# The two gate projections of the forward scan as seven block products for each pair of chunks, with the block sums of the input and of the weights built in the backward pass

## The chip, the core and the metric

The kernel runs on one core of a Trainium2 chip. Its time is that of one execution on the device, in microseconds (us). The engines are named as in the profile: PE (TensorE, matmuls; PEld is its weight load), DVE (VectorE), ACT (ScalarE), POOL (GpSimd) and SP (SyncE, here a queue of DMAs alone). Each engine works through its own instructions in order.

## The reference

One layer of a bidirectional hybrid encoder over 4096 tokens of width 1024, batch 1. Cut to what matters here (`mlstm` stands for the chunkwise mLSTM of one direction, chunks of 128 tokens, 4 heads of 128):

```python
hn = rms_norm(x, norm_w)
qk_a, v_a, o_a, z_a, g_a, q_b, k_b, v_b, z_b = split(hn @ w_in)   # 1024, 512, 512, 512, 16, 512, 128, 128, 512
q_a, k_a = split(silu(centred_depthwise_conv(qk_a, conv_w, conv_b)))
h = sigmoid(o_a) * (mlstm(q_a, k_a, v_a, forward) + mlstm(q_a, k_a, v_a, backward))
h = h * rsqrt(mean(h * h, per head) + EPS) * mhn_w
y_a = h * silu(z_a)
y_b = windowed_gqa(q_b, k_b, v_b, sink, rel_bias) * silu(z_b)
out = rms_norm(x + concat(y_a, y_b) @ w_out, final_norm_w)
```

`o_a` is `hn` times columns 1536 to 2048 of `w_in`, `z_a` is `hn` times columns 2048 to 2560. These two are the gate projections that the change is about.

## The kernel before

Every matmul in float32 is made of three passes at a shorter format: an operand is split into a high part and a low remainder, and PE adds low by high, high by low and high by high into one bank of PSUM. The split costs two instructions, a copy that rounds (ACT) and a subtract (DVE, some on POOL).

The program has four stages.

**First pass** (to about 588 us). Norm, transposes, the windowed attention of group B. It leaves the normalised input, transposed and split, in DRAM as `xT_d`.

**Second pass, the backward scan** (`pass2`, to about 1167 us). Eight blocks of 512 tokens, from the last to the first, four chunks each. Per block PE does the v projection of the four chunks (96 matmuls of 128x512), then the K projections (m = 4 to 7, one for each head) and the Q projections (m = 0 to 3). Behind each of these eight, `qkproj` runs the convolution: ACT evicts into U (L936), POOL copies the four columns shared with the neighbouring block from and into a small tile `hl` (L944, L945), ACT takes the first tap (L948), DVE four more (L950), ACT the tanh (L952), DVE the product (L953). During the Q projections `place` mixes in the transposes of K (`ktp`, L991) and the updates of the state (`kvp`), which need weighed values: `weigh` forms them on POOL and DVE, half each (L1004), then ACT (L1006) and DVE (L1007). POOL also issues the transfers of the state to DRAM (`kf_d`, `cb_d`). The input of a block is eight tiles `xb`, loaded by SP during the block before.

**Third pass, the forward scan** (`pass3`, to about 1679 us). 32 chunks. For each, `proj` makes `op` and `zp`, two times eight K tiles times three matmuls of 128x512 (L1262), in two PSUM banks that take turns (tag `pj`). Behind `op`, ACT takes the tanh (L1270); behind `zp`, ACT the tanh and DVE a product with the bank (L1272). The operands are `xs` tiles, loaded for two chunks at a time from `xT_d`. Among these matmuls `interleave` spreads the scan's own pieces: `heads` (L1214, L1215, the numerators `num`), `yout` (L1249, the transposes `yp` of a chunk's finished heads `hs`), `scores` (L1190, S). `weigh_q` multiplies the weights W by q on DVE (L1204), `state` carries CC forward (L1197), `decays` masks and exponentiates E (POOL L1178, ACT L1182). From num to yp a chunk runs through DVE L1224 to L1226, ACT L1229, DVE L1230, L1234, ACT L1238, DVE L1239, POOL L1240 and DVE L1242.

**Tail.** The z gate of group B for blocks 0 to 7 (`zunits`; L158 to L160, block 0 inside chunk 31 of the scan), and from 1861 us the output projection, which already computes two row blocks by two column blocks with seven products in place of eight (L1443, sums at L1457).

The order on PE is that of the code. The order on the other engines is set by a scheduler with its own estimates; `tc.high_priority(offset=EV)` draws evictions forward, `behind` puts an instruction after another one. Tiles of one tag take turns in a fixed number of buffers, and a load waits until the last reader of its buffer is through. Tiles `x4` (`xtile`) and the weights `w8` (`wtile`) are such rings, shared by all stages.

## Time and profile before

| | us |
|---|---|
| runs | 2188.42, 2188.40, 2185.29; median 2188.40 |
| the profiled execution | 2188.4 |
| its span, first to last instruction | 2182.1 |
| second pass, from about | 588 to 1167 |
| one of its blocks | 74.5 |
| third pass, from about | 1167 to 1679 |
| output projection, PE | 1861.4 to 2172.7 |

The profile is one execution, with the busy time of each engine, tables by stretches of time, and groups of instructions by line, engine, tiles and shape (`out<-in`, partitions x elements, count, busy us, mean ns, then the idle time before them and who ended it). A chain of waits goes back from the last instruction. Line numbers are those of the kernel before.

### The profile page before, as it was taken

What the parts mean: (1) busy time and instruction counts of PE and PEld (TensorE: products, weight loads), DVE (VectorE), ACT (ScalarE), POOL (GpSimd) and SP (SyncE); (2) the same over time, 40 slices, a digit from 0 to 9 for tenths busy, and PEclk for the clock granted to TensorE, in tenths of its full rate; (3) what the DMA queues carried; (4) which work ended last, traced back from release to release, by engine and by line L of the source; (5) the groups of instructions that cost most, each with busy time, mean ns of one, the idle gap of its engine ahead of it and who ended that gap; (6) DMA issues with size and microseconds to landing.
All of it is one profiled execution on the core that took longest, in us unless ns stands there. A gap on an engine that the chain in (4) does not pass through costs nothing. (4 is left out here: it accounts for less than half of the span.)

```text
span 2182.1 us, 34919 instructions
## 1 busy us (share of the span) xinstructions
PE 2156.9 (99%) x12226; PEld 1872.4 (86%) x12226; DVE 1416.9 (65%) x3041; ACT 1079.3 (49%) x2650; POOL 567.7 (26%) x918
## 2 busy tenths in 40 slices
PE   8999999999999999999999999999999999999998
PEld 7999999999898888888888888888888888888886
DVE  7678787788686566556567655555554443777786
ACT  7788788787554344334344544444443321333333
POOL 3555465550031121121112211121211111112222
PEclk9999999999999999999999999999999999999999
DMA  9655455332342454144357887677676998667775
GB/s 277 158 171 147 128 173 122 130 124 64 102 148 78 141 163 135 62 160 160 113 163 230 290 259 238 211 253 225 214 238 188 329 359 283 181 177 191 193 191 147
DMA packets 249132, 398.96 MB, mean 183 GB/s; under 512 B 21979, under 2 KB 128475, under 8 KB 248956
## 3 DMA queue, kind: packets, MB, share of 16 engines
q1 hardware_dynamic: 220544, 303.50, 45.4%
q0 software_dynamic: 28176, 92.96, 13.6%
q8 instruction: 96, 1.57, 0.3%
q14 instruction: 80, 0.66, 0.1%
q10 hardware_dynamic: 236, 0.27, 0.1%
HBM read 275.99 MB, written 120.67 MB: 182 GB/s over the span
## 5 line engine op out<-in xcount | busy, mean ns | idle before, releaser
L932 PE MATMUL up<-xb,w 128*128 128x512 f32 x1344 | 338.4, 396 | 0.0
L1443 PE MATMUL o<-wo,yo 128*128 128x512 f32 (+1 forms) x1356 | 312.8, 393 | 0.0
L1443 PEld LDWEIGHTS o<-wo,yo 128*128 128x128 f32 x1356 | 253.2, 188 | 59.7
L932 PEld LDWEIGHTS up<-xb,w 128*128 128x128 f32 x1344 | 243.8, 188 | 47.2
L950 DVE SCALAR_TENSOR_TENSOR qk<-U,cw,qk 128x512 f32<-128x512 f32 x256 | 189.2, 752 | 91.1 <-ACT qk L948 85.8
L548 PE MATMUL qp<-xT,wqb 128*128 128x256 f32 x1536 | 242.4, 288 | 0.1
L548 PEld LDWEIGHTS qp<-xT,wqb 128*128 128x128 f32 x1536 | 214.2, 190 | 8.7 <-DVE wqb L319 0.5
L1262 PE MATMUL op<-w,xs 128*128 128x512 f32 x720 | 202.3, 408 | 0.0
L1262 PE MATMUL zp<-w,xs 128*128 128x512 f32 x720 | 187.9, 401 | 0.7 <-DVE z L1272 0.7
L905 PE MATMUL v2p<-w,xb 128*128 128x512 f32 x672 | 157.6, 395 | 0.0
L1262 PEld LDWEIGHTS zp<-w,xs 128*128 128x128 f32 x720 | 130.9, 189 | 27.4 <-DVE z L1272 1.1
L414 DVE TENSOR_TENSOR pt<-tp,pt 128x512 fp32r<-128x512 f32 x188 | 129.1, 687 | 37.7 <-ACT pt L413 35.2
L905 PEld LDWEIGHTS v2p<-w,xb 128*128 128x128 f32 x672 | 126.1, 188 | 30.1 <-DMA xb<-xT_d 0.5
L391 ACT ACTIVATE s<-s,NG 128x320 f32<-128x320 f32 (+1 forms) x256 | 139.8, 548 | 11.4 <-DVE NG L389 10.8
L1262 PEld LDWEIGHTS op<-w,xs 128*128 128x128 f32 x720 | 126.7, 189 | 21.4
L413 ACT CAST pt<-tp 128x512 fp32r<-128x512 f32 x188 | 110.5, 588 | 69.9 <-PE tp L411 67.6
L382 DVE CUSTOM_DVE_ANT_0 s<-sp,G 128x320 f32<-128x320 f32 (+1 forms) x256 | 122.2, 478 | 32.6 <-PE sp L379 29.9
L1229 ACT ACTIVATE hs<-num,r 128x128 f32<-128x128 f32 x128 | 47.0, 368 | 174.3 <-DVE r L1226 153.6
L425 PE MATMUL op<-pt,v 128*128 128x512 f32 x376 | 120.6, 402 | 5.9 <-DVE ab L438 5.8
L379 PE MATMUL sp<-kk,q 128*128 128x320 f32 (+2 forms) x512 | 118.8, 313 | 0.7 <-DVE kk L501 0.6
L411 PE MATMUL tp<-ident,s 128*128 128x128 f32 x752 | 113.2, 273 | 0.3 <-DVE pt L414 0.2
L1252 POOL DMA_DIRECT2D y_d<-ya x32 | 19.4, 607 | 329.8 <-ACT ya L1251 181.8
(275 smaller groups left out, 4480.5 us busy)
## 6 DMA issues: line engine op xcount, KB each, us to landing
xc<-xT_d SPq DMA_DIRECT2D x64, 512.0 KB, 8.1
xs<-xT_d SPq DMA_DIRECT2D x120, 256.0 KB, 6.6
xT_d<-xT POOLq DMA_DIRECT2D x104, 256.0 KB, 5.0
xb<-xT_d SPq DMA_DIRECT2D x48, 514.0 KB, 8.0
E<-m_d SPq DMA_DIRECT2D x64, 256.0 KB, 4.9
W<-w_d SPq DMA_DIRECT2D x64, 256.0 KB, 5.9
y<-y_d SPq DMA_DIRECT2D x32, 512.0 KB, 3.4
out<-xr POOLq DMA_DIRECT2D x31, 512.0 KB, 3.7
```

What stands on the lines that cost most here:

```text
L379: nc.tensor.matmul(sp[:, lo:hi], qt, kk[:, kv, z, col - 128 + lo:col - 128 + hi], start=(z == 0), stop=(z == 1))
L382: nc.vector.tensor_tensor_reduce(out=s[:, lo:hi], in0=sp[:, lo:hi], in1=bias[0][:, kv * 2 + m, lo - 64 * half:hi - 64 * half], op0=ALU.add ...
L391: LAST["act"] = nc.scalar.activation(ps[g][:, kept(g)], ps[g][:, kept(g)], AF.Exp, bias=ng[:, g:g + 1], accum_out=rs[:, g:g + 1])
L411: nc.tensor.transpose(tp[:, g * 128:(g + 1) * 128], ps[g][:, j * 128:(j + 1) * 128], c.ident)
L414: nc.vector.tensor_sub(pt[:, 1, :], tp, f32(pt[:, 0, :]))
L425: nc.tensor.matmul(op, vt, pt[:, z, :], start=(i == 0 and z == 0), stop=(i == len(js) - 1 and z == 1))
L548: nc.tensor.matmul(qp, wq[k // 2][:, k % 2, w, m * 128:m * 128 + 128], x[k], start=(k == 0 and j == 0), stop=(k == KT - 1 and j == 2))
L905: nc.tensor.matmul(vp, a, wv[k // 2][:, k % 2, m, :], start=(k == 0 and j == 0), stop=(k == KT - 1 and j == 2))
L932: nc.tensor.matmul(up[:, 0:hi - lo], w[k // 2][:, k % 2, a, cs], x, start=(k == 0 and j == 0), stop=(k == KT - 1 and j == 2))
L950: nc.vector.scalar_tensor_tensor(acc, U[:, t:t + 512], cw[:, cm, t:t + 1], acc, ALU.mult, ALU.add)
L1262: nc.tensor.matmul(P[nm], XS[n](a, k), w[:, m, :], start=(k == 0 and j == 0), stop=(k == KT - 1 and j == 2))
L1443: nc.tensor.matmul(p, a[:, z, k, :], w[k // 2][:, k % 2, m, lo:hi], start=k == 0 and z == 1, stop=k == 3 and z == 0 and m == 0)
```

## The change

For chunks 2j and 2j+1, K halves A (k = 0 to 3) and B (k = 4 to 7), the inputs x0A, x0B, x1A, x1B and the weights oA, oB, zA, zB form a product of two by two blocks. It is computed from seven products of one sum of inputs and one sum of weights each, 12 matmuls of 128x512 per product (4 K tiles, 3 passes):

| product | input | weight | added into |
|---|---|---|---|
| 0 | x0A | oA | copied |
| 1 | x1A + x1B - x0A | zB - zA + oA | u = P1 + P0 |
| 2 | x0B | oB | o of chunk 2j = P2 + P0 |
| 3 | x1A + x1B | zA - oA | z = P3 + u |
| 4 | x0A - x1A | zB - zA | z of chunk 2j+1 = P4 + z; u = P4 + u |
| 5 | x0B - x1A - x1B + x0A | zB | z of chunk 2j = P5 + z |
| 6 | x1B | oB - zB + zA - oA | o of chunk 2j+1 = P6 + u |

- Backward pass: `xunit`, eight times per block, forms the input sums on POOL (six adds, two of 256 columns and four of 128) and writes them to `xo_d` by a POOL transfer of 448 KB; `wunit`, four times in each of blocks 6 to 3, forms the weight sums (two SP loads, two ACT scalings, four POOL adds, one POOL transfer to `wt_d`). `opweights` loads and splits 14 weight tiles (ACT copy and DVE subtract of 128x1024 each), twelve of them in block 0, in place of eight tiles of `wgroup`. In block 0 the last two Q projections are now mixed as in the others.
- Forward scan: `pair` in place of `proj`, 42 matmuls per chunk; `op_load` and `op_split` load and split each input sum (ACT copy; subtract on DVE for even products, on POOL for odd ones). `evict` copies P0 on ACT, adds the others on DVE, and takes the tanh from SBUF.
- E tiles now come from the ring `x4`; lq, lk and lkf have one buffer in place of two.
- The z weights of group B are loaded and split in chunk 29, the z units of block 0 begin in chunk 30 (30 of 32 units there), in pairs of two banks.

Counts of instructions go from 11580 to 11388 on PE, from 3043 to 3215 on DVE, from 2205 to 2361 on ACT, from 920 to 1496 on POOL, from 978 to 1002 on SP.

The core of the diff:

```diff
+        def xunit(b, z):
+            i, kk = divmod(z, 4)
+            j = 2 * b + i
+            u = xtile(c, [128, 8, 128], F32, f"u{j}_{kk}")
+            add = lambda o, x, y, op: nc.gpsimd.tensor_tensor(out=o, in0=x, in1=y, op=op)
+            for k, sl in ((kk, slice(0, 8, 7)), (kk + 4, slice(2, 7, 4))):
+                h, l = [f32(v).rearrange("p (e t) -> p e t", e=2) for v in xv(b, k, 2 + 256 * i, 258 + 256 * i)]
+                add(u[:, sl, :], h, l, ALU.add)
+            add(u[:, 3], u[:, 7], u[:, 6], ALU.add)
+            add(u[:, 1], u[:, 3], u[:, 0], ALU.subtract)
+            add(u[:, 4], u[:, 0], u[:, 7], ALU.subtract)
+            add(u[:, 5], u[:, 2], u[:, 1], ALU.subtract)
+            nc.gpsimd.dma_start(c.xo_d[j, :, :, kk * 128:kk * 128 + 128].rearrange("i p t -> p i t"), u[:, 0:7])
...
             for pair in () if b == 7 else ((3, 2), (1, 0)):
...
+                more(False)
             if b == 0:
-                c.next_weights(0)
+                for i in range(2):
+                    for j in range(2):
+                        opweights(c, i, j)
             for m in range(4, 8):
                 for u in flat(qkproj(b, m)):
                     u()
+                if b < 7:
+                    more(m % 2)
...
+            else:
+                at += [(z / 96, lambda: more(True)) for z in (5, 20)]
...
+        def op_split(g):
...
+            nc.scalar.copy(t[:, 0], st)
+            (nc.gpsimd if g % 7 % 2 else nc.vector).tensor_tensor(out=t[:, 1], in0=st, in1=f32(t[:, 0]),
+                                                                   op=ALU.subtract)
...
+            def mm(i, k, a):
+                g = 7 * j + i
+                if k == 0 and a == 0:
+                    P[i] = c.ps("pj", [128, 512], f"P{j}_{i}")
+                z, m = ((1, 0), (0, 1), (0, 0))[a]
+                nc.tensor.matmul(P[i], operand(g, z, k), c.wt[i][k // 2][:, k % 2, m, :],
+                                 start=k == 0 and a == 0, stop=k == 3 and a == 2)
+                if k == 3 and a == 2:
+                    evict(i)
...
-            fill = (proj(m) if n else p1[24:]) if m < NCH else []
+            fill = take(42)
+            if n == NCH - 2:
+                c.XZ = [load_xt(c, 0, 0, "xc", k) for k in range(KT)]
+                zs = zunits(c, ztiles, 0)
+                fill, zs = fill + zs[:30], zs[30:]
+            if m == NCH:
+                fill = zs
```

Here `more(w)` issues the next `xunit` and, where `w` is set and the block is one of 6 to 3, the next `wunit`.

POOL's queue in the second pass, block 3, around the first weighed values; before (U and hl are the convolution's, wvr the weighed values, v2 the values):

```order
L944 COPY U3_4_10809<-hl4_10219 128x4
L945 COPY hl4_10219<-U4_3_10522 128x4
L1004 TENSOR_TENSOR wvr15_10968<-v2_15_10740,TM_8462 128x4x129
L910 MEMSET v2_11_11357 128x4
L1004 TENSOR_TENSOR wvr14_11050<-v2_14_10747,TM_8462 128x4x129
L910 MEMSET v2_10_11364 128x4
L1004 TENSOR_TENSOR wvr13_11123<-v2_13_10798,TM_8462 128x4x129
L910 MEMSET v2_9_11415 128x4
L944 COPY U3_5_10849<-hl4_10219 128x4
```

The same place now (u are tiles of input sums, wu of weight sums, L892 and L905 their adds, L900 and L914 their transfers, L966 the halo copy):

```order
L900 DMA xo_d_83<-u7_0_11347 128x7x128
L900 DMA xo_d_83<-u6_2_11243 128x7x128
L892 TENSOR_TENSOR u7_1_11394<-xb3_1_10925 128x2x128
L892 TENSOR_TENSOR u7_1_11394<-xb3_5_11008 128x2x128
L900 DMA xo_d_83<-u6_3_11290 128x7x128
L1025 TENSOR_TENSOR wvr15_11414<-v2_15_11118,TM_8464 128x4x129
L905 TENSOR_TENSOR wu3_1_11402<-wu3_1_11402 128x128
L892 TENSOR_TENSOR u7_1_11394<-u7_1_11394 128x128 x2
L966 COPY U3_5_11251<-hl4_10509 128x4
```

Adds and transfers now stand between the halo copies and ahead of the weighed values; two of the three weighed values have moved behind the copy for U3_5.

DVE's queue in the third pass, around a chunk's finished heads; before (chunk 19, `z20<-z20,zp20` empties a bank of `pj`):

```order
L1230 SCALAR_TENSOR_TENSOR hs19_16462<-num19_2_16475,r19_1_16488,hs19_16462 128x128 x2
L1234 SCALAR_TENSOR_TENSOR hs19_16462<-o19_16347,hs19_16462 128x512
L1192 TENSOR_TENSOR E20_16098<-S20_16543,E20_16098 128x512 x2
L1239 TENSOR_SCALAR ss3_19_16497<-ss3_19_16497 128x4
L1204 TENSOR_TENSOR W22_16562<-W22_16562,lq22_16534 128x1024
L1242 SCALAR_TENSOR_TENSOR hs19_16462<-hs19_16462,ss3_19_16497,z19_16394 128x128 x2
L1272 SCALAR_TENSOR_TENSOR z20_16559<-z20_16559,zp20_16514 128x512
```

Now (chunk 18; P10_1 and P10_2 are banks of `pj` of pair 10, L1331 their sums, L1291 a split):

```order
L1331 TENSOR_TENSOR u10_17335<-P10_1_17299,z20_17295 128x512
L1254 SCALAR_TENSOR_TENSOR hs18_17240<-num18_2_17257,r18_1_17271,hs18_17240 128x128
L1291 TENSOR_TENSOR op74_17400<-xr10_4_17297,op74_17400 128x512
L1258 SCALAR_TENSOR_TENSOR hs18_17240<-o18_17042,hs18_17240 128x512
L1228 TENSOR_TENSOR W20_17178<-W20_17178,lq20_17328 128x1024
L1331 TENSOR_TENSOR o20_17385<-P10_2_17339,z20_17295 128x512
L1263 TENSOR_SCALAR ss3_18_17280<-ss3_18_17280 128x4
```

Two sums that empty banks and a split stand among the heads' steps; W is now multiplied two chunks ahead of the finished heads in place of three, and a bank's sum stands right behind it.

PE at the end of the third pass, around chunk 31's transposes; before (zbp0 are the z units of block 0):

```order
L1249 MATMUL yp30_18405<-ident_83,hs30_18169 128x128 x4
L158 MATMUL zbp0_2_18392<-xc0_4_18272,w3_22_13219 128x512
...
L160 MATMUL zbp0_2_18392<-xc0_7_18278,w3_23_13220 128x512
L158 MATMUL zbp0_3_18432<-xc0_0_18264,w3_20_13217 128x512
...
L160 MATMUL zbp0_3_18432<-xc0_1_18266,w3_20_13217 128x512
L1249 MATMUL yp31_18443<-ident_83,hs31_18321 128x128 x4
L158 MATMUL zbp0_3_18432<-xc0_2_18268,w3_21_13218 128x512
```

Now:

```order
L152 MATMUL zbp0_2_19414<-xc0_7_19269,w3_3_19209 128x512
L1238 MATMUL num31_2_19505<-CC31_18901,W31_19064 128x129
L1239 MATMUL num31_2_19505<-lv31_19067,E31_18898 128x129
L1238 MATMUL num31_2_19505<-CC31_18901,W31_19064 128x129
L1239 MATMUL num31_2_19505<-lv31_19067,E31_18898 128x129
L1273 MATMUL yp30_19545<-ident_85,hs30_19310 128x128 x4
L1273 MATMUL yp31_19553<-ident_85,hs31_19496 128x128 x4
L150 MATMUL zbp0_3_19426<-xc0_7_19269,w3_3_19209 128x512
```

Before, 18 matmuls of the z units stand between the two transposes; now none, and the last numerators of chunk 31 lie directly ahead of them.

More of the change, by code (lines that the diff above doesn't have):

```diff
@@ L1028, in pass2, with more @@
         for b in range(7, -1, -1):
+            XU = [lambda z=z, b=b: xunit(b, z) for z in range(8)]
+            def more(w):
+                if XU:
+                    XU.pop(0)()
+                if w and WU and 0 < b < 7:
+                    wunit(WU.pop(0))
             for pair in () if b == 7 else ((3, 2), (1, 0)):
@@ L1284, in pass3 @@
+        load(0, ("k", "q"))
+        for nm, b in (("u", 1), ("o", 2), ("z", 3), ("th", 1), ("hs", 2)):
+            small(nm, b, nm)
+        op_load(1)
         load(0, ("e", "w", "cc", "v", "kf"))
         nc.gpsimd.memset(CCs[0][:, :, 0, :], 0.0)
+        for j in range(2):
+            opweights(c, 6, j, wk)
+        TZ["t"] = c.qth
         with behind(c, TZ["q", 0]):
-            load(1, ("e", "w", "cc", "q", "k"))
-        with behind(c, c.qth):
-            decays(0)
+            load(1, ("e", "w", "cc"))
@@ L1290, in pass3, with take @@
+        decays(0)
         weigh_q(0)
-        load(1, ("v", "kf"))
-        load(2, ("x", "e", "q", "k", "cc"))
-        p0 = proj(0)
-        p1 = proj(1)
-        for u in p0 + p1[:24]:
-            u()
+        stream = [u for j in range(NCH // 2) for u in pair(j)]
+        def take(n):
+            out = []
+            while n and stream:
+                u = stream.pop(0)
+                n -= getattr(u, "cost", 1.0) > 0
+                out.append(u)
+            return out
+        for u in take(72):
+            u()
```

229 lines of the change are left out of this document (124 added, 105 removed).

## The prediction

> **What bounds the kernel now.** I read the page's busy line and slices first, then the chain of waits, then a table by stretches, and only then the groups.
>
> ```profile
> PE 2156.9 (99%) x12226; PEld 1872.4 (86%) x12226; DVE 1416.9 (65%) x3041; ACT 1079.3 (49%) x2650; POOL 567.7 (26%) x918
> ...
> PEclk9999999999999999999999999999999999999999
> ...
> DVE  7678787788686566556567655555554443777786
> ...
> POOL 3555465550031121121112211121211111112222
> ```
>
> TensorE (PE) is busy 99% of the span at an undisturbed clock, so any matmul that goes is time, as long as nobody else makes PE wait. DVE has a third free, POOL three quarters: these two have to carry what the change adds. The chain (start, duration, what) and the table by stretches (us; then PE, weight load, DVE, ACT, POOL busy; clock; DMA share; GB/s):
>
> ```profile
> 1223.25 2.10 PE zp L1262 x9
> ...
> 1255.28 2.08 PE zp L1262 x9
> ...
> 1861.44 311.23 PE o L1443 x1344
> ...
> 700.00:1113.00 413.00, 413.00 (x1961) 341.64 (x1960) 250.73 (x386) 162.18 (x297) 84.89 (x187) 1.00 0.43 140
> 1113.00:1167.00 54.00, 53.32 (x260) 43.72 (x259) 43.25 (x69) 28.69 (x55) 11.93 (x24) 1.00 0.41 123
> ...
> 1200.00:1660.00 460.00, 460.00 (x2641) 397.88 (x2641) 247.46 (x700) 208.62 (x681) 85.34 (x119) 1.00 0.77 242
> ...
> 1861.00:2182.00 321.00, 313.09 (x1358) 253.23 (x1356) 237.82 (x388) 103.99 (x194) 68.41 (x95) 0.99 0.66 178
> ```
>
> The forward scan (1200 to 1660) is PE from end to end. The two zp rows lie two chunks apart: 32.03 us for a pair. The output projection, already seven products with DVE sums between them, runs 1344 matmuls in 311.23 us, 0.2316 us each, with DVE 74% busy: a product scheme of this kind can keep PE full, there with no scan beside it.
>
> **1. Matmuls removed.** The two gate projections are these groups:
>
> ```profile
> L1262 PE MATMUL op<-w,xs 128*128 128x512 f32 x720 | 202.3, 408 | 0.0
> L1262 PE MATMUL zp<-w,xs 128*128 128x512 f32 x720 | 187.9, 401 | 0.7 <-DVE z L1272 0.7
> L1262 PE MATMUL zp<-w,xb 128*128 128x512 f32 x48 | 12.8, 405 | 0.0
> L1262 PE MATMUL op<-w,xb 128*128 128x512 f32 x48 | 11.5, 395 | 0.0
> ```
>
> That is 1536; seven of eight leave 1344. The 192 that go are worth 192 x 0.2316 = 44.5 us (the 408 ns of one is its passage through the pipeline, not its spacing). All of it is on the path. A pair of chunks should shrink from 32.03 to 32.03 - 12 x 0.2316 = 29.25 us.
>
> **2. Block sums in the backward pass, on POOL.** 64 input units (eight per block of four chunks) and 16 weight units (four per block in blocks 6 to 3). The nearest prices:
>
> ```profile
> L276 POOL TENSOR_TENSOR xT<-xraw,xT 128x512 fp32r<-128x512 f32 x52 | 57.0, 1097 | 98.7 <-ACT xT L275 83.0 <-ACT pt L413 7.6 <-PE sp L379 7.6
> ...
> L533 POOL TENSOR_TENSOR G<-vg,gb 128x4 f32<-128x4 f32 x128 | 21.8, 205 | 16.6 <-DVE vg L523 15.4
> ...
> L1004 POOL TENSOR_TENSOR wvr<-v,TM 128x516 f32<-128x516 f32 x28 | 41.7, 1488 | 100.0 <-ACT v L911 85.9 <-PE kv L159 6.4 <-ACT w L104 4.9
> L1097 POOL DMA_DIRECT2D y_d<-zb x28 | 21.0, 754 | 126.8 <-DVE zb L1096 126.0 <-DVE y L1410 0.7
> L1534 POOL DMA_DIRECT2D xr<-x x30 | 31.0, 1033 | 49.2 <-DVE ss L1547 29.5 <-DVE xr L1457 17.6 <-DMA y<-y_d 1.8
> ```
>
> Between L533 and L276 an add grows by (1097 - 205)/508 = 1.76 ns a column: 0.42 us for 128 columns, 0.65 for 256. An input unit is 2 x 0.65 + 4 x 0.42 plus a transfer issue. No row has an issue of 896 short rows; 0.75 (L1097) and 1.03 (L1534) bound it, and I take 0.95, nearer the longer: 3.9 us. With L1004's slope (2.51 ns, disturbed by DVE) it is 4.7. A weight unit is 4 x 0.42 + 0.95 = 2.6. A block of the backward pass lasts 74.5 us, POOL's share of it now 84.89/413 x 74.5 = 15.3. With eight input units it is 46.7; in blocks 6 to 3, with weight units, 57; at the upper price 65. It fits, but POOL goes from a fifth to three quarters, and its queue holds what PE needs through others: the halo copies ahead of the convolution, half of the weighed values (wvr), two transfers per chunk.
>
> Two things can cost. [...]
>
> ```profile
> 965.10 0.69 DVE L1004 TENSOR_TENSOR wvr<-v,TM 128x516 f32<-128x516 f32 x1 [3.29 <-ACT v L911]
> 965.15 1.56 POOL L1004 TENSOR_TENSOR wvr<-v,TM 128x516 f32<-128x516 f32 x1 [5.53 <-ACT v L911]
> ...
> 780.68 1.16 POOL L1004 TENSOR_TENSOR wvr<-v,TM 128x516 f32<-128x516 f32 x1 [0.41 <-PE up L932]
> 780.84 1.55 DVE L1004 TENSOR_TENSOR wvr<-v,TM 128x516 f32<-128x516 f32 x1
> ```
>
> Whichever starts first runs at its own pace (0.69, 1.16); the other takes that much longer (1.56, 1.55). [...]
>
> Second, the slack. Of a block these rows give the end of the last K head's convolution, the transpose that needs it, and the period:
>
> ```profile
> 719.33 22.58 PE L905 MATMUL v2p<-w,xb 128*128 128x512 f32 x96
> ...
> 770.06 0.69 DVE L953 SCALAR_TENSOR_TENSOR qk<-th,qk 128x512 f32<-128x512 f32 x1
> ...
> 774.81 0.60 PE L991 MATMUL ktp<-ident,qk 128*128 128x128 f32 x4
> ...
> 793.84 6.41 PE L905 MATMUL v2p<-w,xb 128*128 128x512 f32 x27
> ...
> L945 POOL COPY hl<-U 128x4 f32<-128x4 f32 x64 | 20.6, 321 | 208.3 <-ACT U L936 208.3
> ```
>
> The slack is 774.81 - 770.75 = 4.06 us. The last head has four steps on DVE; held by one 256-column add each they lose 4 x 0.65 = 2.6 us, inside the slack. The adds mostly run in the 22.58 us of the v projection: some 24 adds, six issues and one wvr, 24 x 0.45 + 6 x 0.95 + 1.5 = 18 us, stand ahead of the second head's halo copy, which isn't due until that head's eviction, 22.6 + 2 x 5.6 (24 more matmuls each) = 33.8 us into the block. So the queue is ahead by some 15 us there, and by my walk through it 6 to 8 us at the last head. I take 0.7 us a block for seven blocks, **5 us**; the ends are 0 and 20 (3 us a block).
>
> **3. Weights.** Before, 16 scaled splits of this kind; now 14 tiles of 1024 columns, twelve in the last block of the backward pass.
>
> ```profile
> L105 DVE SCALAR_TENSOR_TENSOR w<-w_1s,nw,w 128x512 fp32r<-128x512 f32 x8 | 5.7, 742 | 0.0
> ```
>
> For their subtract stands L1204 below (1.23 us), so DVE has 14 x 1.23 = 17 instead of 16 x 0.74 = 12 us of it, in a stretch (1113 to 1167) where it is 80% busy. Each product needs its own two tiles, and the slots come free only as the old weights are done. I take **2 us**, between 0 (products come 2.8 us apart) and 6.
>
> **4. The scan's DVE.** Per pair there come seven PSUM adds and four splits, 128x512 each (the other three splits go to POOL); tanh counts stay.
>
> ```profile
> L1457 DVE TENSOR_TENSOR xr<-o,xr 128x512 f32<-128x512 f32 x64 | 43.3, 682 | 2.0 <-PE o L1443 1.9
> L1204 DVE TENSOR_TENSOR W<-W,lq 128x1024 f32<-128x1024 f32 x32 | 39.2, 1225 | 95.5 <-DMA lq<-q_d 83.7 <-DMA lk<-k_d 10.5 <-DMA W<-w_d 0.8
> ...
> 1388.33 0.33 SPq L1155 DMA_DIRECT2D lq<-q_d  x1
> ...
> 1394.60 1.23 DVE L1204 TENSOR_TENSOR W<-W,lq 128x1024 f32<-128x1024 f32 x1 [2.87 <-DMA lq<-q_d]
> ```
>
> DVE now has 247.46/460 x 32.03 = 17.2 us a pair; 11 x 0.682 = 7.5 more make 24.7 of 29.25, 84%. POOL's three splits (1.1 us each, as L276) and its powers collide with DVE's two-input steps, nearly half of its work: 1 to 3 us a pair, so about 90%. What matters more is the order. DVE already stands still for q, 2.87 us in the row shown (6.3 us from issue to use). Now q has one buffer, its load starts when S is done, and behind W in DVE's queue stands the sum that empties the third product's bank. Counted from the end of S: W starts at 6.4, ends at 7.7, the sum ends at 8.4; PE wants the bank at 8.95 (15 + 12 matmuls and 12 head products of 0.22, the distance of the first two rows under 5). That is 0.55 us of room in one place of each pair, gone when q lands a little later or DVE is a little behind. I take 0.6 us a pair, 16 pairs, **10 us**; the ends are 0 and 2.2 a pair (35), where DVE's work would be the pair's length.
>
> **5. The scan's end.** The z units of group B now mostly lie in chunk 30, and chunk 31's transposes directly behind chunk 30's, with three matmuls behind its last head. The chain it needs, before:
>
> ```profile
> 1670.28 0.39 PE L1214 MATMUL num<-CC,W 128*128 128x129 f32 x2
> 1670.50 0.39 PE L1215 MATMUL num<-lv,E 128*128 128x129 f32 x2
> ...
> 1677.62 1.13 DVE L1242 SCALAR_TENSOR_TENSOR hs<-hs,ss,z 128x128 f32<-128x128 f32 x4
> ```
>
> From 1670.89 to 1678.75 it takes 7.9 us, of which about 7 are its own steps. PE stood behind 16 or more other matmuls there before; now only chunk 30's transposes (0.5 us) lie between. So 6.5 to 7.5 us of idle PE, and one eviction of the z units inside the chain and their paired banks add 1 to 2: **9 us**, ends 6 and 11.
>
> **Sum.** The profiled execution took 2188.4 (span 2182.1 and 6.3 around it), the median itself. 2188.4 - 44.5 + 5 + 2 + 10 + 9 = 2169.9, so **2170 us**. DMA isn't a term: the sums' 37 MB of writes go where the DMA share is 0.43, and the scan's loads fall by an eighth.
>
> **The rivals.** (a) *Everything hides but the end*: 2188.4 - 44.5 + 6 to 9 = 2150 to 2153. For it speak DVE's 84% and the output projection's full PE at 74%; against it the 0.55 us of room. [...] (c) *Slower: POOL falls behind in the backward pass.* A halo copy later than the 8 + 4 us of room at the last K head holds back convolution, transpose, kv and the next block. At 6 us for each of six blocks, 36 in place of 5, the sum is 2201. It decides where POOL's block exceeds some 70 us; my upper price is 65 before waits for transfers. (d) *The change doesn't cut PE*: excluded, since the program has 192 matmuls fewer; the chain would have to be elsewhere.
>
> **Numbers.** My sum (2157 to 2183): 0.46. (a) 0.25, (b) 0.12, (c) 0.17. About 0.2%, 4.4 us, is what a measurement of this kernel can tell from none. (a) and my sum are faster, with a little of (b): 0.73; no change 0.09, mostly (b); slower 0.18, (c) and the rest of (b). The range takes (a) whole and (b) and (c) up to 2198.
>
> **What would show it.** Matmuls of the products: 1344, nearly gap-free, pairs 29.2 to 30.5 us apart. [...] In the backward pass blocks of 74.5 to 76 us, POOL 60 to 80% busy; ktp waiting for L953 behind the halo copy shows (c). At the end one hole of 6 to 9 us ahead of the last yp. Wrong would be: blocks over 78 us, or no hole at the end.

## The result, and the profile after

The changed kernel takes 2375.59 us (median of four runs, 2374.28 to 2382.61) against 2188.41 us (2185.29 to 2188.96, four runs): a ratio of 1.0868 (95% interval 1.0851 to 1.0884). It is 187 us slower; forecast were 18 us less. The profiled execution took 2375.4, with a span of 2373.7: in span the difference is 191.6 us, since less lies around this one than around that of before. Its page, busy line and slices:

```profile
PE 2171.2 (91%) x12034; PEld 1857.1 (78%) x12034; DVE 1614.1 (68%) x3213; ACT 1145.1 (48%) x2806; POOL 965.8 (41%) x1494
...
PE   8999999999888779879899699999998799999998
...
POOL 2655655420487756774655223232232111112222
PEclk9999999999989989989899899999999899999999
```

The 192 matmuls are gone (12226 to 12034), and yet PE is busy longer; one reason is its clock, granted at 0.93 in the first stretch below, where it was 1.00 before (the last section follows one such fall). Its holes lie in slices 11 to 23, through most of which POOL is now 40 to 80% busy, and in 31 and 32, ahead of the tail. By stretches (us; PE, weight load, DVE, ACT, POOL busy; clock; DMA share; GB/s), the backward pass and the steady forward scan:

```profile
700.00:1250.00 550.00, 474.85 (x2137) 386.16 (x2136) 356.79 (x413) 183.31 (x348) 357.80 (x626) 0.93 0.54 168
1400.00:1860.00 460.00, 423.01 (x2363) 347.95 (x2361) 315.97 (x811) 244.96 (x745) 127.33 (x144) 1.00 0.70 218
```

In neither is an engine full, though PE was at 100% in both before. So PE waits for others by turns, and the question is for whom. From the starting times of matmuls I read this table (us; a chunk is the distance of two `yp`, over 26 chunks):

| | before | after | cost | my term |
|---|---|---|---|---|
| start of block 6 (first v projection) | 644.6 | 667.6 | 23 | |
| blocks 6 to 1, mean of one | 74.5 | 91.9 | 104 | |
| block 0 to its last kv | 74.6 | 83.2 | 9 | 5 for all three |
| first gate matmul to first `yp` | 39.1 | 65.5 | 26 | 2 |
| a chunk of the scan, 26 of them | 16.04 | 16.75 | 18 | -44.5 + 10 for all 32 |
| `yp` of chunk 28 to the output projection | 205.5 | 215.8 | 10 | 9, less its chunks' matmuls |

These make 190 of the 191.6 us; the rest lies between them. The last of the 26 chunks, which reaches into chunk 29 with its z weights of group B, takes 21.49 us; the other 25 take 16.56.

**Backward pass.** The groups that matter there:

```profile
L972 DVE SCALAR_TENSOR_TENSOR qk<-U,cw,qk 128x512 f32<-128x512 f32 x256 | 263.2, 1037 | 51.6 <-ACT qk L970 30.4 <-POOL U L966 15.2 <-POOL wu L905 1.2
L927 PE MATMUL v2p<-w,xb 128*128 128x512 f32 x672 | 173.2, 420 | 59.4 <-ACT v L933 59.4
L892 POOL TENSOR_TENSOR u<-u 128x128 f32<-128x128 f32 x256 | 138.9, 561 | 0.6
```

The convolution's steps on DVE (L972, L950 before) took 751 ns in the median before, and 1.21 us at most. Their median is still that, but the longest now takes 12.15 us (minimum/median/maximum in ns; before, then after):

```profile
L950 DVE SCALAR_TENSOR_TENSOR qk<-U,cw,qk x256: 734/751/1206, 595.0 to 1171.7; 128x512 f32<-128x512 f32 x128
...
L972 DVE SCALAR_TENSOR_TENSOR qk<-U,cw,qk x256: 734/752/12149, 596.0 to 1313.1; 128x512 f32<-128x512 f32 x128
```

The v projection, which had no hole before, waits 59.4 us for its bank to be emptied (ACT, L933). How the two belong together is in the timeline of block 3, a little of each engine:

```profile
952.49 14.67 DVE L972 SCALAR_TENSOR_TENSOR qk<-U,cw,qk 128x512 f32<-128x512 f32 x5
...
953.82 12.48 DVE L972 SCALAR_TENSOR_TENSOR qk<-U,cw,qk 128x512 f32<-128x512 f32 x2
...
959.40 2.50 POOL L892 TENSOR_TENSOR u<-u 128x128 f32<-128x128 f32 x6
...
963.49 0.96 POOL L900 DMA_DIRECT2D xo_d<-u  x1
...
967.09 0.68 DVE L975 SCALAR_TENSOR_TENSOR qk<-th,qk 128x512 f32<-128x512 f32 x1
...
967.80 0.63 ACT L974 ACTIVATE th<-qk 128x512 f32<-128x512 f32 x1 [10.01 <-DVE qk L975]
...
968.33 1.06 ACT L933 COPY v<-v2p 128x512 f32<-128x512 f32 x2
...
968.95 3.35 PE L927 MATMUL v2p<-w,xb 128*128 128x512 f32 x7 [10.28 <-ACT v L933]
```

While POOL runs its small adds, six in 2.50 us, DVE needs 14.67 us for five steps, 12.48 of them for two (3.30 and 9.26). The second of the two ends at 966.30, under POOL's last adds in this stretch; the transfer that POOL issues at 963.49 did not let it go on. ACT stands 10.01 us in its queue at a tanh that waits for a step of DVE behind the held one (L975); the emptying of PE's bank is queued behind that tanh on ACT, and PE waits 10.28.

Five such holes of 9.2 to 12.2 us stand in these six blocks, and each follows one step of DVE held for 9.2 to 12.1 us: four are the convolution's, one is the product L975. Over the six blocks PE is busy 472.4 of 551.2 us, where it was busy all of 447.0 before with the same 2115 matmuls. So of the 104 us lost here, 79 are idle PE, 54 of them in the five holes, and 25 are matmuls that take longer, at a granted clock of 0.92 in the mean.

At the first block, PE stands still earlier, for the weighed values of block 7:

```profile
652.12 0.88 DVE L1025 TENSOR_TENSOR wvr<-v2t,TM 128x516 f32<-128x516 f32 x1 [6.62 <-POOL u L892]
...
655.54 1.05 ACT L1027 CAST wvh<-wvr 128x1032 fp32r<-128x1032 f32 x1 [12.40 <-POOL wvr L1025]
656.64 0.28 PEld L150 LDWEIGHTS kv<-wvh,kt 128*128 128x128 f32 x1 [13.97 <-ACT wvh L1027]
```

POOL's half of them stands in its queue behind the sums, and PE waits 14 us. But the sums' adds are not all of it. Other waits there (590 to 668 us) are for transfers:

```profile
DVE wvl L1028 <- DMA xo_d<-u: 6.2, 1, 6.2
...
ACT kf L1042 <- DMA kf_d<-kf: 5.6, 1, 5.6
```

The remainder of the weighed values (`wvl`) takes its buffer from the same ring as the sums, and waits until a sum's transfer has landed; the state's transfers to `kf_d` are issued by POOL among the sums. With no adds at all (e4, below) ACT waits 6.18 us there for `kf_d`, and block 6 still starts 11.8 us late.

**Start of the scan.** First gate products, in order of time:

```profile
1303.08 2.95 PE L1342 MATMUL P<-wt,xb 128*128 128x512 f32 x12
...
1313.20 2.47 SPq L977 DMA_DIRECT2D q_d<-qk  x2
...
1317.84 1.99 ACT L1121 CAST wt<-ws 128x1024 fp32r<-128x1024 f32 x2 [0.48 <-DMA q_d<-qk]
1318.11 0.43 SPq L1283 DMA_DIRECT2D xr<-xo_d  x1
...
1321.05 0.62 ACT L1290 CAST op<-xr 128x512 fp32r<-128x512 f32 x1 [1.22 <-DMA xr<-xo_d]
1321.76 1.78 POOL L1291 TENSOR_TENSOR op<-xr,op 128x512 fp32r<-128x512 f32 x1 [11.25 <-ACT op L1290]
...
1323.59 5.30 PE L1342 MATMUL P<-wt,op 128*128 128x512 f32 x12 [17.56 <-POOL op L1291]
```

On SP the load of the second product's input (1318.11) comes behind those of the last weights and behind the stores of the last convolved q (1313.20), for which SP waits until DVE is through with the convolution (5.1 us at the longest). On ACT its split comes behind the last weights' splits. PE stands still for 17.56 us.

**The scan.** PE's waits from 1340 to 1800 us (who waits for whom: us in all, times, longest):

```profile
PE P L1342 <- ACT z L1324: 13.2, 13, 1.2
PE P L1342 <- DVE u L1327: 8.5, 13, 0.7
PE P L1342 <- DVE z L1331: 4.3, 12, 0.4
PE P L1342 <- DVE r L1248: 4.2, 7, 1.2
PE P L1342 <- DVE o L1331: 2.4, 7, 0.8
```

These 460 us hold 13.7 pairs. Before, the scan had no such wait. Once a pair each, a product waits for the copy of P0 out of its bank (L1324), for the second sum of P4 (L1327), for that of P3 (L1331), and so on: 32.6 us in these rows, 2.4 a pair, at the starts of five of the seven products. The pair takes 33.5 us where by my price its matmuls would take 29.25. Of these 4.25, 2.7 are idle PE (37.0 of the 460 us from 1400 to 1860, above). The other 1.6 are not gaps: PE is busy 30.8 us a pair, at a clock of 1.00. Why its work takes longer than the price stays open.

### The profile page after: what moved, and what is told of

Its sections match the earlier page's. It is cut to its first block, busy times and chain, and to the rows that moved or that the text cites. A ratio compares the mean times of both kernels' runs of the same rounds, so it can differ in the third digit from the quotient of the medians.

```text
span 2373.7 us, 35774 instructions
## 1 busy us (share of the span) xinstructions
PE 2171.2 (91%) x12034; PEld 1857.1 (78%) x12034; DVE 1614.1 (68%) x3213; ACT 1145.1 (48%) x2806; POOL 965.8 (41%) x1494
## 4 chain that ended last, share of the span: by engine, by line
PE 41%; DMA 19%; DVE 15%; issue 10%; POOL 8%; ACT 6%; SPq 1%; POOLq 0%; ACTq 0%; DVEq 0%
PE qp L540 7%; DMA xr<-xo_d 5%; PE up L954 5%; DVE qk L972 5%; DMA xr<-x 4%; POOL u L892 4%; PE op L417 3%; PE v2p L927 3%; PE tp L403 3%; PE sp L371 3%; PE zbp L150 3%; PE zbp L152 3%; PE zbp L151 3%; DMA lq<-q_d 2%; PE o L1533 2%
## 5 line engine op out<-in xcount | busy, mean ns | idle before, releaser
L1342 PE MATMUL P<-wt,op 128*128 128x512 f32 x1320 | 372.1, 414 | 56.1 <-POOL op L1291 17.6
L954 PE MATMUL up<-xb,w 128*128 128x512 f32 x1344 | 344.6, 401 | 0.0
L1342 PEld LDWEIGHTS P<-wt,op 128*128 128x128 f32 x1320 | 231.7, 191 | 122.6 <-issue 22.9
L972 DVE SCALAR_TENSOR_TENSOR qk<-U,cw,qk 128x512 f32<-128x512 f32 x256 | 263.2, 1037 | 51.6 <-ACT qk L970 30.4
L927 PE MATMUL v2p<-w,xb 128*128 128x512 f32 x672 | 173.2, 420 | 59.4 <-ACT v L933 59.4
L927 PEld LDWEIGHTS v2p<-w,xb 128*128 128x128 f32 x672 | 136.2, 204 | 95.2 <-ACT v L933 62.5
L383 ACT ACTIVATE s<-s,NG 128x320 f32<-128x320 f32 (+1 forms) x256 | 139.8, 548 | 11.8 <-DVE NG L381 11.2
L1291 POOL TENSOR_TENSOR op<-xr,op 128x512 fp32r<-128x512 f32 x48 | 62.1, 1295 | 192.9 <-ACT op L1290 192.9
L892 POOL TENSOR_TENSOR u<-u 128x128 f32<-128x128 f32 x256 | 138.9, 561 | 0.6
L150 PE MATMUL zbp<-xc,w 128*128 128x512 f32 x256 | 103.5, 404 | 5.4 <-DVE o L1148 5.4
L1290 ACT CAST op<-xr 128x512 fp32r<-128x512 f32 x110 | 67.8, 616 | 80.8 <-DMA xr<-xo_d 79.6
```

The lines of the kernel that those rows point to most:

```text
L150: nc.tensor.matmul(out, wl, xh, start=first, stop=False)
L383: LAST["act"] = nc.scalar.activation(ps[g][:, kept(g)], ps[g][:, kept(g)], AF.Exp, bias=ng[:, g:g + 1], accum_out=rs[:, g:g + 1])
L892: add = lambda o, x, y, op: nc.gpsimd.tensor_tensor(out=o, in0=x, in1=y, op=op)
L927: nc.tensor.matmul(vp, a, wv[k // 2][:, k % 2, m, :], start=(k == 0 and j == 0), stop=(k == KT - 1 and j == 2))
L954: nc.tensor.matmul(up[:, 0:hi - lo], w[k // 2][:, k % 2, a, cs], x, start=(k == 0 and j == 0), stop=(k == KT - 1 and j == 2))
L972: nc.vector.scalar_tensor_tensor(acc, U[:, t:t + 512], cw[:, cm, t:t + 1], acc, ALU.mult, ALU.add)
```

## Experiments in the backward pass

Each of the four ran once beside the kernel before (2190.75 us there), with a profile. They differ in what a unit's adds become.

**e1_memset** replaces each add by a memset of like length on POOL, so POOL's queue has as many instructions and POOL is nearly as busy; the block sums are then left out.

```diff
-            add = lambda o, x, y, op: nc.gpsimd.tensor_tensor(out=o, in0=x, in1=y, op=op)
+            def add(o, x, y, op):
+                nc.gpsimd.memset(u[:, 0:3] if done else u[:, 0:7], 0.0)
+                done.append(1)
```

> The changed kernel, with every add of the block sums on POOL replaced by a POOL memset of about the same length (first one 896 columns, the others 384) in the same tiles; the sums are left out, so the gate products use zeros. POOL is busy about as long, but reads nothing from SBUF. Theory A (a DVE instruction with two SBUF inputs that has to wait for POOL waits for a whole run of POOL adds, and ACT and PE behind it): the 9 to 12 us holes in the v projection go, blocks of the backward pass fall from 89-95 us to 75-79, the whole time by 85 to 115 us to about 2260-2290. Rival B (POOL's queue is simply too long, and halo copies and weighed values come late): blocks stay at 88 us or more, time 2350-2380. Rival C (buffers of the shared ring are held by the transfers of the sums): the 14 us hole in the first block stays and blocks stay above 85 us.

**e2_dve_adds** puts the adds on DVE (`nc.vector` for `nc.gpsimd`).

> The changed kernel with all adds of the block sums on DVE in place of POOL (about 2 us of DVE a unit, 16 us a block). Theory A: no run of POOL reads is left, blocks fall to 75-82 us, time to 2260-2300. Rival B: the same, so this run doesn't tell A from B. Rival C: blocks stay above 85 us. If DVE with 16 us more becomes the bound of a block: also above 85, but then DVE is busy over 90% there.

**e3_gap** leaves the adds on POOL, strictly one behind another, with a memset of four columns between any two.

```diff
+            def add(o, x, y, op):
+                with behind(c, c.last):
+                    a = nc.gpsimd.tensor_tensor(out=o, in0=x, in1=y, op=op)
+                with behind(c, a):
+                    c.last = nc.gpsimd.memset(c.gap, 0.0)
```

> The changed kernel with a POOL memset of 4 columns (0.1 us) forced between any two adds of the block sums; all else is computed as before. POOL gets longer by some 6 us a block. Theory A in its narrow form (DVE gets no turn because the next POOL add is already there): a short instruction without SBUF reads lets DVE in, long waits of single DVE instructions (4 to 12 us) shrink to 1-2 us, blocks 76-84 us, time 2270-2320. Rival B: POOL longer, blocks 92-100 us, time 2380-2430.

**e4_no_adds** leaves the sums out; one memset remains for each unit, beside its transfers.

> The changed kernel with the adds left out but for one memset per unit (896 columns), the transfers kept; the gate products use zeros. What is left of the loss in the backward pass is then transfers, ring and weights. Theory A and rival B: blocks at 74.5-77 us, time about 2255-2275, and what the forward scan loses (about 16.75 us a chunk instead of 14.65, start and end) stays. Rival C: the first block's hole and blocks above 85 us stay.

| | time | start of block 6 | mean block | POOL busy in it | longest step | steps over 0.75 us, in all |
|---|---|---|---|---|---|---|
| after | 2375.6 | 667.6 | 91.9 | 59.8 | 12.15 | 74.1 |
| e1_memset | 2265.1 | 658.7 | 76.6 | 52.4 | 2.30 | 10.9 |
| e2_dve_adds | 2287.9 | 657.2 | 79.8 | 25.5 | 2.08 | 7.1 |
| e3_gap | 2318.9 | 665.9 | 83.3 | 65.1 | 2.52 | 36.9 |
| e4_no_adds | 2281.2 | 656.4 | 79.6 | 32.7 | 2.00 | 2.8 |

Blocks are 6 to 1. The last column is what the convolution's 256 steps (L972 of after) take beyond 0.75 us each. The convolution's group in e1 and in e3, and the v projection's in e1:

```profile
L980 DVE SCALAR_TENSOR_TENSOR qk<-U,cw,qk 128x512 f32<-128x512 f32 x256 | 198.4, 789 | 66.4 <-ACT qk L978 61.3 <-DMA xb<-xT_d 1.1 <-POOL u L895 0.4
...
L935 PE MATMUL v2p<-w,xb 128*128 128x512 f32 x672 | 157.5, 395 | 0.0
```

```profile
L981 DVE SCALAR_TENSOR_TENSOR qk<-U,cw,qk 128x512 f32<-128x512 f32 x256 | 224.6, 891 | 48.2 <-ACT qk L979 40.9 <-POOL cl L897 3.9
```

A POOL queue of as many instructions, nearly as busy, that doesn't read SBUF gives back 15 of 17.4 us a block, and PE's holes at the v projection are gone (0.0). e3 has the same adds, with something between: POOL is even busier than in after (65.1 us a block), yet the blocks are 8.6 us shorter and the steps of 9 to 12 us are gone; each of many steps loses a little instead. So neither the length of the queue nor the halo copies in it make most of the loss, which was my rival (c); what the adds do to DVE makes it. In total 110 of the 187 us go with the adds being POOL adds (2375.6 to 2265.1, the latter one run).

What stays is not explained by them: 2 to 5 us a block, and 12 us at the first one, even with no adds (e4). In e1 block 6 alone has 9 of these us (83.5); the five after it take 75.2 on average. e4 does less than e1 and has longer blocks, 79.6 where 74.5 to 77 was expected; the scheduler's order differs between these kernels, and I did not separate its part.

## What a step of DVE waits for

That an instruction of POOL holds up a two-input step of DVE was in my reckoning (L1004 on DVE, 0.69 us ahead of POOL's half and 1.55 behind it), with one add for one step. Three programs of their own measured it. In each, POOL runs a row of N adds of 128 columns, and DVE does one step like the convolution's (L972: 128x512, two inputs in SBUF).

**m1_port**: N from 0 to 32, all adds into one tile; memsets, copies and wide adds for comparison.

> A small kernel of its own; it computes nothing of the layer and only fills the output. One DVE step like the convolution's (128x512, two SBUF inputs) is started just behind the start of a POOL run of N instructions, for N = 0, 1, 2, 4, 8, 16, 32 adds of 128 columns; then 16 adds with a 4-column memset between any two, 16 memsets, 16 copies, 1 and 4 adds of 1024 columns, 16 adds with the DVE step's first input in PSUM, and 16 adds with four DVE steps. Theory A (DVE waits for the whole run): the step takes 0.74 + 0.42 N, thus 1.2 us at N = 1, 4.1 at 8, 7.5 at 16, 14 at 32; with memsets between 1.2-1.6; with 16 memsets and with PSUM 0.74; with 4 adds of 1024 columns 8-9. Rival D (DVE waits for one POOL instruction, as the pairs of the profile before suggested): 1.2 us at every N from 1 on, 2.6 with adds of 1024 columns, and in the last case each of the four steps is held once.

```profile
24.92 17.24 POOL L61 TENSOR_TENSOR p<-p,p 128x128 f32<-128x128 f32 x32
25.07 0.85 DVE L80 SCALAR_TENSOR_TENSOR acc<-x,sc,acc 128x512 f32<-128x512 f32 x1
```

Even a run of 32 costs the step one add's rest, 0.1 us; a single add of 1024 columns costs 2 us (2.73). That would excuse my one add, but these adds stand 0.54 us apart (17.24/32), and the kernel's 0.41: its units are interleaved, so neighbours don't depend on each other. Hence

**m2_port**: the same with adds into one tile, two or eight tiles in turn, a chain, 256 columns, and memsets between.

> A program of its own, not the scan: GpSimd runs a row of N adds of 128 columns while VectorE does one step like the convolution's (128x512, 0.75 us alone). The rows differ in where the adds write: one tile (as in m1_port), two tiles in turn, eight in turn (independent, as adds of different units are in the changed kernel), a chain in which each add reads the one before, 256 columns wide, or a memset of 4 columns between. Theory A' (a step waits until GpSimd leaves a gap, and adds that don't depend on each other leave none): adds into eight tiles follow at about 0.41 us, and the step lasts about 0.75 + 0.41 N, so 4 us at N = 8, 7.3 at N = 16, 13.9 at N = 32; into one tile 0.85 as in m1_port; with the memsets 0.85 to 1.3. Rival D (a step waits for one add at most, wherever the adds write; the long steps of the changed kernel have another cause): 0.85 to 1.2 us in every row, and GpSimd's adds are pushed apart instead. In between (the step gets its turn after some number k of adds) would be steps that level off as N grows.

```profile
32.08 7.06 POOL L62 TENSOR_TENSOR o<-p,p 128x128 f32<-128x128 f32 x16
32.23 0.85 DVE L84 SCALAR_TENSOR_TENSOR acc<-x,sc,acc 128x512 f32<-128x512 f32 x1
...
39.23 13.75 POOL L62 TENSOR_TENSOR o<-p,p 128x128 f32<-128x128 f32 x32
39.38 12.87 DVE L84 SCALAR_TENSOR_TENSOR acc<-x,sc,acc 128x512 f32<-128x512 f32 x1
```

With eight tiles, the step beside a run of 32 lasts 12.87 us, in all three repetitions 12.87 to 13.27. This is a step as long as the kernel's, made in isolation. But beside 16 and 8 it lasts 0.85, so "0.75 + 0.41 N" was wrong as a rule.

**m3_phase**: runs of 24, the step 0 to 3 us into the run; then dependent adds, memsets between, and other kinds of step.

> A program of its own again: GpSimd runs 24 adds of 128 columns into eight tiles in turn, and VectorE does one step that comes later and later in that run, behind a copy from PSUM to PSUM of 0 to 2048 columns; then, behind a copy of 1024 columns, the run with dependent adds (one tile, a chain), the run with memsets between, and other kinds of VectorE instruction of the same size. In m2_port a step that came 0.15 us after the first add was held 12.9 us in the run of 32 and not at all in the runs of 8 and 16. Theory A'' (the step gets in only if it comes before adds have begun to overlap; once GpSimd's adds follow at 0.41 us, each begun before the last has ended, no change of adds lets it in): behind 0 columns 0.85 or about 10 us; behind every copy of more than about 0.5 us the step lasts from where it stands to the end of the run, so about 9.5 us behind 512 columns, 9 behind 1024, 7.5 behind 2048; 0.85 to 1.3 with dependent adds or memsets wherever it comes. Rival (the hold of 12.9 us belongs to the length of the run, and runs under 32 let the step in after one add): 0.85 to 1.3 in every row. For the kinds: a step that reads PSUM, and a copy or a scaling of one SBUF tile, aren't held if the hold needs two SBUF inputs (0.7 to 0.8), and are held about 9 us if it doesn't.

Two runs that follow each other:

```profile
6.71 10.36 POOL L63 TENSOR_TENSOR o<-p,p 128x128 f32<-128x128 f32 x24
6.78 0.93 DVE L91 SCALAR_TENSOR_TENSOR acc<-x,sc,acc 128x512 f32<-128x512 f32 x1
...
17.16 10.46 POOL L63 TENSOR_TENSOR o<-p,p 128x128 f32<-128x128 f32 x24
...
17.44 9.04 DVE L91 SCALAR_TENSOR_TENSOR acc<-x,sc,acc 128x512 f32<-128x512 f32 x1
```

Of the 33 runs of independent adds with this step, 17 held it 7 to 10 us, to within the last three adds of the run, and 16 let it in at the next change of adds (0.74 to 1.06), wherever in the run it came. Both expectations, arrival and length, fell. In this program the two outcomes alternate: a held step always follows a run whose step was let in. DVE's report, for which POOL's next run has a wait, comes some 8 us before it is due in the one case, and 1 us or less in the other. But in m2_port the run of 256-column adds held its step (5.88 us) right behind a held one, two times of three, and the runs of 8 and 16 let theirs in behind one that was let in. What decides it stays open. Shown is: with dependent adds or memsets between, no step was held (0.74 to 0.87, nine of nine).

The kinds of step, each behind a run whose step was let in:

```profile
161.37 0.74 DVE L83 SCALAR_TENSOR_TENSOR acc<-ps,sc,acc 128x512 f32<-128x512 f32 x1
...
171.37 0.56 DVE L85 COPY acc<-x 128x512 f32<-128x512 f32 x1
...
181.63 8.56 DVE L87 TENSOR_TENSOR acc<-x,acc 128x512 f32<-128x512 f32 x1
```

With one input from PSUM (L83, 0.74 us) the step isn't touched; a copy gets in (0.56 us); a sum of two SBUF tiles is held 8.56 us. (A scaling, 0.48 us, came behind a held run, so it tells nothing.) The held step stays through many adds that start after it: in the second of the two runs above some 20, at 9.04 us with an add every 0.44 us (10.46/24).

## Experiments in the scan

These build on e2_dve_adds, which leaves nothing out, and ran once each; first four, beside 2186.5 us for the kernel before.

**f1_split_dve**: the products' input splits all on DVE, none on POOL.

> On top of the kernel with the block sums on DVE (e2, 2288 us; its forward scan takes 16.74 us a chunk, 65 us from the first gate matmul to the first transposes of heads): all seven splits of a pair's input sums on DVE, none on POOL. [...] Theory Q (with two banks, the sum that empties a bank comes too late because it stands in queues behind other work of ACT and DVE): DVE gets 2 us more a pair, a chunk stays at 16.5-17.0.

**f2_three_banks**: a third bank for the products, for which S and `yp` share one.

```diff
-        c.psum({"pj": 2, "n": 2, "c": 1, "y": 1})
+        c.psum({"pj": 3, "n": 2, "c": 1})
```

> On top of e2: three PSUM banks for the seven products in place of two; to make room, S and the heads' transposes share one bank. Theory Q: the waits at the starts of products (3.4 us a pair) mostly go, a chunk falls from 16.74 to 14.9-15.6, the time by 30 to 50 us to about 2240-2258; a new wait of S on the eviction of the transposes may take back up to 0.3 us a chunk. [...]

**f3_ends**: the first input sums loaded early, into tiles of the shared ring; at the end the z units one by one in one bank each, ten of them in chunk 30 instead of thirty.

```diff
-                zs = zunits(c, ztiles, 0)
-                fill, zs = fill + zs[:30], zs[30:]
+                zs = zunits(c, ztiles, 0, False)
+                fill, zs = fill + zs[:10], zs[10:]
```

> On top of e2, two edits in stretches that don't touch: (start) the first loads of input sums go into the shared ring and are issued ahead of the loads of k and q, so that they don't wait for the buffers of the backward pass; (end) the z units of block 0 one after the other instead of in pairs, 10 of them in chunk 30 and 22 in chunk 31, so that 6 matmuls and more stand between the last two transposes. If the 17.6 us hole at the start is that load: first gate matmul to first transposes falls from 65 to 45-50 us. If it is something else: stays above 60. End: the hole ahead of the last transposes (9.8 us) falls below 4, and from the 29th transposes to the output projection 216 becomes 206-210 us. Chunks in between stay at 16.7.

**f4_copy_dve**: P0 copied out of its bank by DVE instead of ACT.

> On top of e2: the first product's bank is emptied by a DVE copy in place of an ACT copy (which stands behind the eight exponentials of E, 2.4 us). If ACT's queue is what costs at the third product: its wait of 1.2 us a pair goes, a chunk falls by 0.3-0.6 to 16.1-16.4. If DVE's queue is as late: stays at 16.6-16.9.

**g1_forward** (before: 2188.14) joins f3 and f2, with `yp` placed behind the S of its chunk, the first split drawn forward and the last weights later. **g2_all** adds weight rows loaded one call ahead and the sums of block 7 earlier.

> On top of f3 (2268 us: sums on DVE, z units of block 0 one by one): three banks for the products, S and the transposes in one bank as in f2, but with the transposes 9 matmuls behind S in place of 4 ahead of it; and at the start the first split of an input sum is issued ahead of other work of ACT, the last two weight tiles after two products. Theory Q (bank waits are what the chunk loses): a chunk falls from 16.7 to 14.7-15.3, and the start, first gate matmul to first transposes, from 64 to 42-50 us; time 2185-2225. If DVE's or ACT's work as such is the bound: a chunk stays above 16.

> On top of g1: in the backward pass the weight rows are loaded one call ahead of their scaling, and the eight input units of the first block are issued before the state updates in place of among them. If ACT waits for those loads ahead of the evictions of v (holes of 4 us in blocks 6 to 4), blocks 6 to 3 fall from 80-81 to 76-78; if the first block's 11 us hole is the ring (weighed values wait for transfers of sums), the v projection begins at 645-650 in place of 657. Time 10 to 30 us below g1's; about 2165-2200, that is near the time before.

| | time | first gate matmul to `yp` | chunk | `yp` of 28 to output |
|---|---|---|---|---|
| before | 2188.4 | 39.1 | 16.04 | 205.5 |
| e2_dve_adds | 2287.9 | 64.6 | 16.74 | 216.3 |
| f1_split_dve | 2279.7 | 63.5 | 16.61 | 215 |
| f2_three_banks | 2297.2 | 61.2 | 17.14 | 211 |
| f3_ends | 2268.3 | 64.2 | 16.71 | 201.6 |
| f4_copy_dve | 2295.3 | 65.1 | 17.05 | 216.4 |
| g1_forward | 2256.8 | 67.9 | 16.45 | 192.9 |
| g2_all | 2270.2 | 68.7 | 16.33 | 193.8 |

Taking the adds off POOL doesn't change the scan (16.75 to 16.74), as it should not. With POOL's splits on DVE a chunk is 0.13 us shorter (f1), so collisions with them are at most a small part of the loss. The third bank takes away every wait of a product for its bank that this view shows, and gives it back elsewhere: PE's waits from 1340 to 1800 us in f2, then in g1:

```profile
PE S L1214 <- ACT ya L1275: 38.7, 19, 3.3
```

```profile
PE yp L1273 <- DVE E L1216: 31.8, 19, 3.1
```

In f2, S waits for `yp` to be emptied, in g1 `yp` for DVE to have read S, 2 to 3 us a pair in both. The third bank was taken from S and `yp`, so what one stream gets another loses. f2's chunk was to fall to 14.9-15.6 and rose to 17.14, with the granted clock at 0.95 (1330 to 1700 us); g1's was to fall to 14.7-15.3, and at 16.45 it is above the 16 that I had put for DVE's or ACT's work as the bound. So it is shown that products wait for their banks, but not that more banks would end the loss: whether there are too few, or DVE and ACT empty them too late in their queues, these runs don't separate. Even the best mean chunk, 16.33, is longer than before. In f4, with the copy on DVE, the wait for it (12.2 us in e2) goes, and those for the sums of DVE (L1331) grow from 3.4 and 1.8 us in e2 to 7.5 and 8.9 in the same stretch, with 11.2 at u; its chunk, 17.05, is longer than either theory had it.

The end is mended by f3: 14.7 us less than e2, below even the kernel before; the longest wait ahead of transposes there is 4.1 us. The start is not. PE's hole there in f3, then in g1:

```profile
1235.29 0.79 PE L1342 MATMUL P<-wt,op 128*128 128x512 f32 x1 [19.39 <-POOL op L1291]
```

```profile
1238.06 2.50 PE L1343 MATMUL P<-wt,op 128*128 128x512 f32 x5 [18.31 <-POOL op L1292]
```

f3 issues the load of the second product's input at 1207.79, 5 us ahead of the first gate product, and the hole is longer than before: its split comes at 1228.22 on ACT, behind the convolution's last tanhs and the last weights, and at 1233.97 on POOL, behind a mask that waits 13.56 us for the load of E. In g1 and g2 that split is in time, and the hole (18.31 and 18.57 us) stands two products later, ahead of the fourth, whose input is loaded only at 1229.74 in g1. So it isn't this one load; the first loads and splits of the scan stand in several queues behind the end of the convolution, and none of these orders is without the hole.

g2 missed both of its expectations: blocks 6 to 3 take 80.1 us, not 76 to 78, and block 6 starts at 668.5, not at 645 to 650. I found no version that beats the kernel before; the best, g1, is 69 us over it.

## Why the prediction was wrong

- *Matmuls removed, -44.5.* The count was right; the price supposes that PE stays full, and it didn't: a pair went from 32.03 to 33.5 us, with PE busy 30.8 of them where the price leaves 29.25.
- *Backward pass, 5 (ends 0 and 20).* This step failed first and furthest: 136 us, with blocks of 91.9 us where I had named 78 as a sign of being wrong. The price of a unit was near: an input unit is 2 x 0.738 + 4 x 0.561 + 0.948 = 4.7 us as measured, my upper price, and the issue was taken as 0.95. What failed is "held by one 256-column add each they lose 4 x 0.65 = 2.6 us". It was an estimate, and no run of the kernel shows that term: a step was held by whole runs of adds, up to 12.15 us, and e1, without the adds, has 92 of the six blocks' 104 us back. The rows I had quoted showed POOL instructions that stand alone; none showed what a row of them does, and so the upper end of 3 us a block was no bound.
- *The walk through POOL's queue* asked whether POOL was in time. It mostly was (e1: as many instructions in the queue, 76.6 us a block). What I left out is ACT's queue: the tanh that waits for the held convolution has the eviction of the v projection's bank behind it. With that, a late convolution isn't covered by the 4.06 us of slack at the last head; it stops PE at the next bank.
- *Rival (c)*, slower by the backward pass, had the right place and the wrong mechanism and price: 36 us in six blocks for POOL's lateness, against 104, most of it from DVE held. Its condition, POOL over some 70 us a block, did not come (59.8).
- *Weights and start, 2 (ends 0 and 6).* It was 26. I priced DVE's time and left out the path of the first input sums, their loads on SP and their splits on ACT and POOL, which stand behind the last of the convolution and the weights; nothing covers the hole of 17.56 us. Moving the one load (f3) or the one split (g1) only moved the hole.
- *The scan's DVE, 10 (ends 0 and 35).* I expected 0.55 us of room in one place of each pair, at W (27 x 0.2316 + 12 x 0.22 is 8.9 rather than 8.95, so 0.5). The loss is 4.25 us a pair, 68 us in 16; 2.4 of it are waits at the starts of five products, since each bank must be emptied within one product's 12 matmuls. DVE's load was no bound (316 of 460 us, 69%, against my 84%), nor POOL's (127 of 460). The output projection, which I read as proof that such a scheme keeps PE full, has no scan's queue ahead of its sums; I named that difference and gave it no price.
- *The end, 9 (6 to 11).* The hole was there, the size too small; PE's waits in the tail of after:

```profile
PE yp L1273 <- DVE hs L1266: 9.8, 1, 9.8
PE zbp L150 <- DVE o L1148: 5.4, 2, 4.7
```

  The one ahead of the last `yp` is the hole that I forecast. The second row stands where I had 1 to 2 us for the z units' banks. Together they are 15.2; the stretch grew by 10 only, since it has 45 matmuls fewer as well, some 10 us at 0.2316. The 5 us that this leaves stay open.
- *The range.* Its upper end took the price of one add for one step as a bound. It was an assumption.

## What to carry to other kernels

Before work is moved to an idle POOL, ask which two-input SBUF steps DVE does at that time, and who stands behind them in order: here a row of small independent adds held one step for nearly the whole row (12.87 of 13.75 us in m2_port, 12.15 us at the longest in the kernel), and ACT's queue carried that on to PE (waits of 10.01 and 10.28 us). Adds on DVE itself (longest step 2.08 us), a small instruction between (2.52), or an input from PSUM (0.74) avoided the long hold here. A scheme with fewer matmuls but more sums asks that every bank be emptied within one product's time (the waits for banks were 2.4 us a pair here): count that in the queues as they are, and not for the sum alone.

## What was not expected of the hardware

- A DVE step with two SBUF inputs was held up to 12.15 us in the kernel and 12.87 to 13.27 us in isolation by POOL adds of 0.45 us each that follow at 0.41; beside 32 adds 0.54 us apart it took 0.85 us, and as long beside 16 at 0.41.
- After the 17.56 us hole, PE's next twelve matmuls took 5.30 us, against 2.95 for the twelve ahead of it. The granted clock around it (last but two column), in the hole and behind it:

```profile
1305.00:1322.00 17.00, 1.03 (x5) 0.50 (x3) 12.54 (x17) 9.09 (x18) 4.26 (x5) 0.59 0.85 251
1323.00:1329.00 6.00, 5.41 (x14) 4.30 (x15) 0.00 (x0) 0.35 (x1) 1.78 (x3) 0.54 0.94 298
```

  It was 1.00 ahead of the hole (1290 to 1303 us) and again behind those twelve matmuls (1329 to 1333 us). At 0.54 they ran at nearly half their pace, all twelve. This hole thus costs 2.35 us more than itself. Before, the stretches quoted have no such hole of PE, and their clock is 0.99 to 1.00.
